# A streaming encoder step on one core: the tiles that TensorE streams, laid out at one offset within 256 bytes

## The chip, the cores and the metric

The kernel runs on one core of one Trainium2 chip, in one launch. The metric is the device time in microseconds. Three runs of the kernel before took 2901.51, 2903.31 and 2903.32 us; the median is 2903.31 us. TensorE multiplies, VectorE (DVE), ScalarE (ACT) and GpSimd (POOL) do the rest, SyncE (SP) issues most DMAs.

## The reference

A two-layer encoder runs on 288 frames: 256 of a new stream (the prompt) and 32 of a running one (the sample), with D = 2048 channels, all in float32.

```python
for i in range(DEPTH):                                   # two layers
    if i % 2 == 0:  h, v = gmlp_mix(x, w_a_in, ..., w_a_out)      # 2048 -> 4096, spatial gating, 2048 -> 2048
    else:           h, s = retention_mix(x, ..., w_b_in, w_b_out) # 2048 -> 12288, 8 heads, 4096 -> 2048
    x = layer_norm(ALPHA * x + h)
    gate, up = jnp.split(x @ w_ffn_in[i], 2, axis=-1)             # 2048 -> 11264
    x = layer_norm(ALPHA * x + (silu(gate) * up) @ w_ffn_out[i])  # 5632 -> 2048
```

Outputs are the frames, the retention states of both streams and the normalised v rows of the sample.

## The kernel before, in words

Activations lie transposed: channels on the 128 partitions, the 288 frames along the free axis. A matrix of 2048 input channels is cut into blocks of 128 x 128; there are `NBLK` = 512 + 256 + 1536 + 512 + 2 x (1408 + 704) = 7040 of them, and 64 blocks of carried state.

Float32 accuracy comes from pairs. Each weight block and each activation tile is split into a rounded part (`hi`) and the rest (`lo`), and `Core.step` (lines 103 to 105) issues three matmuls for a block: `whi` by `xh`, `whi` by `xl`, `wlo` by `xh`. Each loads its 128 x 128 weights and streams 288 columns of the activation. That makes 3 x 7040 = 21120 matmuls. In three places (`PostNorm.start`, `RAW` = 3 groups of 4 output tiles, 16 blocks each) 290 columns are streamed, two of them for the gain and bias of the norm before: 3 x 3 x 4 x 16 x 3 = 1728 matmuls. The other 19392 stream 288 columns.

The stages follow each other: `a_in` (32 output tiles), `a_out` (16), then for each layer `f_in` and `f_out` in two halves, with `b_in` and `b_out` in two halves between the two layers. For an output tile the loop runs over the input tiles `k` (16 for `a_in`, `b_in`, `f_in`, `a_out`, `b_out`; 22 for `f_out`). Only the first group of `a_in` turns this round: for one `k` it runs over 8 output tiles, so 24 matmuls in a row stream the same two tiles `xh[k]` and `xl[k]` (`Core.group`, `lag=0`).

Weights arrive in the order of use, packed in chunks of 8 blocks (512 KB), through SP's queue. For each chunk ACT rounds (`split`, line 413) and DVE subtracts (line 414). Four chunks are held, each block 512 bytes per partition. PE's order is written out by hand; the other engines follow through semaphores, with moves through DRAM issued by POOL (`to_rows`, lines 422 to 424, and `o_move`).

What TensorE streams are: `xh`, `xl` (the input of a mixer or FFN), `g_sh`, `g_sl` (gated product), `hh`, `hl` (FFN hidden half), `r_oh`, `r_ol` (retention output, four tiles for each of four heads). In the built program their rows of 288 or 292 numbers begin, in each partition:

| tile | start, bytes | step from `k` to `k+1` | start of the rows modulo 256 |
|---|---|---|---|
| `xh` | 61568 | 1168 | 128, 16, 160, 48, 192, 80, 224, 112, 0, 144, 32, 176, 64, 208, 96, 240 for k = 0 to 15 |
| `xl` | 80256 | 1168 | the same |
| `g_sh`, `g_sl` | 131712, 150144 | 1152 | 128 and 0 in turn |
| `hh`, `hl` | 131712, 157056 | 1152 | 128 and 0 in turn |
| `r_oh`, `r_ol` | four places each | 1152 | 32 and 160, or 96 and 224, in turn |

The weight blocks `whi` and `wlo` begin at 128 modulo 256 throughout (`whi` at 28800, `wlo` at 45184, blocks 512 and buffers 4096 bytes apart). The first 16384 bytes of each partition are the scratch of the dynamic DMAs.

Of the kernel before, what the change touches and what calls it, by code (L numbers as in the profile page):

```python
# [10 lines left out]
F32 = mybir.dt.float32  # L11
F32R = mybir.dt.float32r
# [7 lines left out]
P = 128  # L20
D = 2048
KT = D // P
NP = 256
NS = 32
NT = NP + NS
NX = NT + 2
ROW = NT + 4
NR = 3 * NS
HID = 5632
HT = HID // P  # L30
HH = HT // 2
# [377 lines left out]
                       lambda m, ps: evac(m, self.correct(m, ps)), lambda s, g=g: hook(g, s))  # L409


def split(nc, hi, lo, f):
    nc.scalar.copy(hi, f)  # L413
    nc.vector.tensor_tensor(lo, f, hi.bitcast(F32), ALU.subtract)  # L414
# [12 lines left out]
def gmlp(core, cst, x, y, lnp, ins, v_out, load):  # L427
    tc, nc = core.tc, core.nc
    xh, xl = x
    xs = lambda k: (xh[:, k, :NT], xl[:, k, :NT])  # L430
    with ExitStack() as es:
        pool = es.enter_context(tc.tile_pool(name="gm", bufs=1, reuse_waits="tile"))
        sh = pool.tile([P, KT, NT], F32R, name="g_sh")
        tv = pool.tile([P, 4, 9, 4, 32], F32, tag="sl", name="g_tv")
        vp = pool.tile([P, 2, D], F32, name="g_vp")
        vs = y.rearrange("p k n -> p (k n)")[:NS, :D]
        v3 = pool.tile([NR, D], F32R, name="g_v3")
# [26 lines left out]
        rows = [P, P, NS]  # L464
# [65 lines left out]
        def mix(m, u):  # L530
            g = m // 2
            ps = core.bank(f"mix{m}")
            for t in range(2):
                nc.tensor.matmul(ps[:, t * P:(t + 1) * P], vp[:, t, m * P:(m + 1) * P], ws[:, g, :], start=True, stop=True)
            s = pool.tile([P, NT], F32, tag="s", name=f"s{m}", bufs=2)
            two = lambda t: t[:, :NP].rearrange("p (t n) -> p t n", t=2)
            nc.vector.tensor_tensor(two(s), two(ps), bs[:, g:g + 1, :].broadcast_to([P, 2, P]), ALU.add)
            nc.vector.tensor_tensor(s[:, NP:], ms[:, m, :], bs[:, g, :NS], ALU.add)
            nc.vector.tensor_tensor(s, s, u, ALU.mult)
            if m == 0:  # L540
                late["sl"] = pool.tile([P, KT, NT], F32R, tag="sl", name="g_sl")
            split(nc, sh[:, m, :], late["sl"][:, m, :], s)

        late = {}
        core.group("a_in", 0, list(range(KT)), list(range(16, 24)), xs, v_evac, load, lag=0)
        core.tiles("a_in", 0, list(range(KT)), list(range(24, 32)), xs, v_evac, grouped=False)
        core.tiles("a_in", 0, list(range(KT)), list(range(16)), xs, u_evac, grouped=False)
        ln = PostNorm(core, cst, x, y, lnp, 0)
        core.tiles("a_out", 0, list(range(KT)), list(range(KT)), lambda k: (sh[:, k, :], late["sl"][:, k, :]),
                   lambda m, ps: ln.last(m, ps, True))  # L550
    return ln

# [1 line left out]
def ffn(core, cst, x, y, lnp, layer, prev, out=None):  # L554
    tc, nc = core.tc, core.nc
    xh, xl = x
    xs = lambda k: (xh[:, k, :NT], xl[:, k, :NT])
    ln = PostNorm(core, cst, x, y, lnp, 2 * layer + 1, out)
    with tc.tile_pool(name=f"ffn{layer}", bufs=1, reuse_waits="tile") as pool:
        hh = pool.tile([P, HH, NT], F32R, name=f"hh{layer}")  # L560
        hl = pool.tile([P, HH, NT], F32R, name=f"hl{layer}")
        for half in range(2):
            sg = {}

            def evac(m, ps):
                if m < HT:
                    t = pool.tile([P, NT], F32, tag="sg", name=f"sg{layer}_{m}", bufs=4)
                    nc.scalar.activation(t, ps[:, :NT], AF.Silu)
                    sg[m] = t
                else:  # L570
                    j = m - HT
                    i = j - half * HH
                    f = pool.tile([P, NT], F32, tag="hf", name=f"hf{layer}_{j}", bufs=3)
                    nc.vector.tensor_tensor(f, ps[:, :NT], sg.pop(j), ALU.mult)
                    split(nc, hh[:, i, :], hl[:, i, :], f)

            ms = []
            for j in range(half * HH, (half + 1) * HH):
                ms += [j, HT + j]
            if half == 0:  # L580
                prev.start(f"f_in{layer}", ms, evac)
                ms = ms[4 * RAW:]
            core.tiles(f"f_in{layer}", 0, list(range(KT)), ms, xs, evac, grouped=False)
            core.tiles(f"f_out{layer}", half * HH, list(range(HH)), list(range(KT)),
                       lambda k: (hh[:, k, :], hl[:, k, :]),
                       ln.last if half else ln.part)
    return ln


def retention(core, cst, x, y, lnp, prev, ins, st_p_out, st_s_out):  # L590
    tc, nc = core.tc, core.nc
    xh, xl = x
    xs = lambda k: (xh[:, k, :NT], xl[:, k, :NT])
    mm = nc.tensor.matmul
    with ExitStack() as es:
        pool = es.enter_context(tc.tile_pool(name="ret", bufs=1, reuse_waits="tile"))
        oh, ol = {}, {}
        cs = pool.tile([P, 2, NT], F32, name="r_cs")
        zt = pool.tile([P, HEADS, 3], F32, name="r_zt")
        inn = pool.tile([P, HEADS, NS], F32, name="r_inn")  # L600
# [8 lines left out]
        heads = {}  # L609

        def pair(name, h):
            t = pool.tile([P, 4 * NT], F32, tag=f"oh{h % 4}", name=name)
            return t[:, :2 * DV].rearrange("p (t f) -> p t f", t=2)

        def rope(dst, a, b, cos, sin, nm):
            t1 = pool.tile([P, NT], F32, tag="rt1", name=f"rt1{nm}", bufs=1)
# [8 lines left out]
        class Head:  # L625
# [10 lines left out]
            def evac(self, m, ps):  # L636
                h = self.h
                if m < 32:
                    self.ps[m % 2] = ps
                    if m % 2:  # L640
                        turn = lambda p=dict(self.ps): self.turn(m, p)
                        if h == 0:
                            core.after(2, turn)
                        else:
                            turn()
                elif m < 64:
                    i = m % 4
                    if i == 0:
                        self.tv = pool.tile([P, 9, 4, 32], F32, tag=f"ol{h % 4}", name=f"tv{h}")
                    nc.vector.transpose(self.tv[:, :, i, :], ps[:, :NT])  # L650
                    if i == 3:
                        self.v_move()
                else:
                    i = m % 4
                    nc.scalar.activation(self.sg[:, i, :], ps[:, :NT], AF.Silu)
                    if i == 3:
                        core.after(1, lambda: self.o_gate("g"))
# [152 lines left out]
            def o_move(self):  # L810
                h = self.h
                to = pair(f"to{h}", h)
                tz = pool.tile([P, DV], F32, tag="tz", name=f"tz{h}")
                self.of = of = pool.tile([P, 9, 4, 32], F32, tag=f"ol{h % 4}", name=f"of{h}")
                nc.vector.transpose(tz[:NS, :], self.ons[:NS, :])
                nc.vector.transpose(to.rearrange("p t f -> p (t f)"), self.onp.rearrange("p t f -> p (t f)"))
                room = core.room([NT, DV], f"o_room{h}")
                nc.gpsimd.dma_start(room[NP:, :], tz[:NS, :])
                nc.gpsimd.dma_start(room[:NP, :].rearrange("(t p) f -> p t f", p=P), to)
                blocks = room.rearrange("(b s) f -> s b f", s=32)  # L820
                for a in range(4):
                    nc.gpsimd.dma_start(of[32 * a:32 * a + 32].rearrange("p b i s -> p b (i s)"), blocks[:, :, a * P:(a + 1) * P])

            def o_gate(self, what):
                self.open.discard(what)
                if self.open:
                    return
                h = self.h
                view = lambda t: t.rearrange("p i (b s) -> p i b s", s=32)
                nc.vector.tensor_tensor(view(self.sg), self.of.rearrange("p b i s -> p i b s"), view(self.sg), ALU.mult)  # L830
                oh[h % 4] = pool.tile([P, 4, NT], F32R, tag=f"oh{h % 4}", name=f"r_oh{h}")
                ol[h % 4] = pool.tile([P, 4, NT], F32R, tag=f"ol{h % 4}", name=f"r_ol{h}")
                for i in range(4):
                    split(nc, oh[h % 4][:, i, :], ol[h % 4][:, i, :], self.sg[:, i, :])

            def states(self):
                h = self.h
# [24 lines left out]
        for grp in range(2):  # L862
            a, b, c, d = order[4 * grp:4 * grp + 4]
            ms = sum(a + b, []) + c[0] + d[0] + c[1] + d[1]
            if grp == 0:
                prev.start("b_in", ms, evac)
                ms = ms[4 * RAW:]
            core.tiles("b_in", 0, list(range(KT)), ms, xs, evac, grouped=False)
            core.tiles("b_out", 16 * grp, list(range(16)), list(range(KT)),
                       lambda k: (oh[k // 4][:, k % 4, :], ol[k // 4][:, k % 4, :]),  # L870
                       ln.last if grp else ln.part)
    return ln

# [2 lines left out]
def hybrid_step(ctx, tc, ins, outs):  # L876
    nc = tc.nc
    ctx.enter_context(tc.manual_schedule(engines={PE}))
    core = Core(ctx, tc, ins["wpack"])
    cp = ctx.enter_context(tc.tile_pool(name="cp", bufs=1))  # L880
    lnp = ctx.enter_context(tc.tile_pool(name="lnp", bufs=1))
    xh = cp.tile([P, KT, ROW], F32R, name="xh")
    xl = cp.tile([P, KT, ROW], F32R, name="xl")
    y = cp.tile([P, KT, NT], F32, name="y")
    cst = {}
    cst["one2048"] = cp.tile([P, P], F32, name="one2048")
# [111 lines left out]
```

## Time and profile before

| | |
|---|---|
| median of three runs | 2903.31 us |
| profiled execution, its own time | 2903.1 us |
| its span | 2901.3 us |
| PE busy | 2888.0 us |
| DVE busy | 1697.5 us |
| ACT busy | 1241.3 us |
| POOL busy | 141.8 us |
| granted TensorE clock, mean | 0.999 of full speed |

The span runs from the first to the last instruction of the profiled execution; 1.8 us of its own time lie outside. Matmuls overlap in the records: each is shown as about 295 ns long, while the next one starts some 130 ns after it. So the busy time of PE says that there was always a matmul under way, not how fast they follow each other. The rate is read from the distance between starts.

### The profile page before, as it was taken

Reading aid. Unit: us, or ns where it says so; the run is one execution under the profiler, and the core shown is the slowest. Engines: PE = TensorE matmul, PEld = TensorE weight load, DVE = VectorE, ACT = ScalarE, POOL = GpSimd, SP = SyncE. Lnnn points to the kernel's source line nnn. Section 1 sums busy time; section 2 is a strip of 40 time slices with the busy share of each in tenths; the row PEclk is TensorE's granted clock in tenths of the full one; section 3 lists DMA queues with packets and bytes.
Section 4 is the critical chain, followed back from the end, with each engine's and each line's share of the span. In section 5 each row is a group of like instructions: output and inputs, shape, how many; then the busy total and the mean of one; then the engine's idle time right before and its main releaser. Section 6 shows DMA issues by size and latency. Waiting matters only on the chain.

```text
span 2901.3 us, 51390 instructions
## 1 busy us (share of the span) xinstructions
PE 2888.0 (100%) x21568; PEld 2873.1 (99%) x21568; DVE 1697.5 (59%) x2432; ACT 1241.3 (43%) x1642; POOL 141.8 (5%) x241
## 2 busy tenths in 40 slices
PE   9999999999999999999999999999999999999998
PEld 9999999999999999999999999999999999999998
DVE  5677864444444456777755566767854444444455
ACT  5444553333333344554443344444543333333343
POOL 1100000000000000012200111200000000000001
PEclk9999999999999999999999999999999999999999
DMA  8654455554555544567655566755454554555553
GB/s 268 209 172 160 160 167 168 167 167 161 166 167 167 167 161 166 185 201 226 221 190 163 191 209 208 219 188 163 165 165 166 167 167 164 165 166 167 167 167 121
DMA packets 146584, 515.49 MB, mean 178 GB/s; under 512 B 18016, under 2 KB 20336, under 8 KB 146320
## 3 DMA queue, kind: packets, MB, share of 16 engines
q1 hardware_dynamic: 131984, 473.47, 49.5%
q0 software_dynamic: 14224, 38.59, 4.6%
q8 instruction: 168, 2.75, 0.4%
q14 instruction: 64, 0.52, 0.1%
q10 hardware_dynamic: 144, 0.15, 0.0%
HBM read 486.98 MB, written 25.17 MB: 177 GB/s over the span
## 4 chain that ended last, share of the span: by engine, by line
PE 98%; DVE 1%; DMA 0%; issue 0%; POOL 0%; ACT 0%; SPq 0%; DVEq 0%; POOLq 0%
PE af_in L104 13%; PE af_in L103 13%; PE af_in L105 13%; PE ab_in L103 7%; PE ab_in L104 7%; PE ab_in L105 7%; PE af_out L103 7%; PE af_out L105 6%; PE af_out L104 6%; PE ab_out L105 2%; PE ab_out L103 2%; PE ab_out L104 2%; PE aa_in L103 2%; PE aa_in L104 2%; PE aa_in L105 2%; PE aa_out L103 1%
## 5 line engine op out<-in xcount | busy, mean ns | idle before, releaser
L414 DVE TENSOR_TENSOR wlo<-raw,whi 128x1024 fp32r<-128x1024 f32 (+1 forms) x892 | 1085.8, 1219 | 951.7 <-ACT whi L413 947.7
L413 ACT CAST whi<-raw 128x1024 fp32r<-128x1024 f32 (+1 forms) x892 | 931.9, 1046 | 1505.7 <-PE af_in L104 353.5
L104 PE MATMUL af_in<-xl,whi 128*128 128x288 f32 (+1 forms) x2816 | 831.4, 295 | 0.0
L103 PE MATMUL af_in<-xh,whi 128*128 128x288 f32 (+1 forms) x2816 | 829.5, 295 | 0.0
L105 PE MATMUL af_in<-xh,wlo 128*128 128x288 f32 (+1 forms) x2816 | 828.0, 294 | 0.0
L103 PEld LDWEIGHTS af_in<-xh,whi 128*128 128x128 f32 x2816 | 530.6, 188 | 0.0
L105 PEld LDWEIGHTS af_in<-xh,wlo 128*128 128x128 f32 x2816 | 530.0, 188 | 0.0
L104 PEld LDWEIGHTS af_in<-xl,whi 128*128 128x128 f32 x2816 | 529.5, 188 | 0.0
L104 PE MATMUL ab_in<-xl,whi 128*128 128x288 f32 (+1 forms) x1536 | 453.3, 295 | 0.0
L103 PE MATMUL ab_in<-xh,whi 128*128 128x288 f32 (+1 forms) x1536 | 453.2, 295 | 0.0
L105 PE MATMUL ab_in<-xh,wlo 128*128 128x288 f32 (+1 forms) x1536 | 451.7, 294 | 0.0
L103 PE MATMUL af_out<-hh,whi 128*128 128x288 f32 x1408 | 416.1, 296 | 0.0
L104 PE MATMUL af_out<-hl,whi 128*128 128x288 f32 x1408 | 415.2, 295 | 0.0
L105 PE MATMUL af_out<-hh,wlo 128*128 128x288 f32 x1408 | 414.4, 294 | 0.0
L103 PEld LDWEIGHTS ab_in<-xh,whi 128*128 128x128 f32 x1536 | 289.2, 188 | 1.0
L104 PEld LDWEIGHTS ab_in<-xl,whi 128*128 128x128 f32 x1536 | 288.9, 188 | 1.1
L105 PEld LDWEIGHTS ab_in<-xh,wlo 128*128 128x128 f32 x1536 | 289.0, 188 | 0.0
L105 PEld LDWEIGHTS af_out<-hh,wlo 128*128 128x128 f32 x1408 | 265.0, 188 | 0.0
L104 PEld LDWEIGHTS af_out<-hl,whi 128*128 128x128 f32 x1408 | 264.3, 188 | 0.0
L103 PEld LDWEIGHTS af_out<-hh,whi 128*128 128x128 f32 x1408 | 263.9, 187 | 0.0
L103 PE MATMUL aa_in<-xh,whi 128*128 128x288 f32 x512 | 152.5, 298 | 0.4 <-ACT xh L413 0.4
L104 PE MATMUL aa_in<-xl,whi 128*128 128x288 f32 x512 | 152.0, 297 | 0.0
(253 smaller groups left out, 2941.1 us busy)
## 6 DMA issues: line engine op xcount, KB each, us to landing
raw<-in_wpack_dram SPq DMA_DIRECT2D x887, 512.0 KB, 3.4
v_room<-tv POOLq DMA_DIRECT2D x32, 144.0 KB, 4.8
of<-o_room POOLq DMA_DIRECT2D x32, 144.0 KB, 4.4
vw<-v_room POOLq DMA_DIRECT2D x8, 512.0 KB, 6.1
out_st_s_dram<-sso POOLq DMA_DIRECT2D x16, 256.0 KB, 2.8
o_room<-to POOLq DMA_DIRECT2D x8, 512.0 KB, 3.6
out_st_p_dram<-so POOLq DMA_DIRECT2D x16, 256.0 KB, 5.2
y<-in_xT_dram SPq DMA_DIRECT2D x8, 288.0 KB, 5.3
```

The costliest lines, as they stand in the source:

```text
L103: mm(ps[:, :n], hi, xh, start=first, stop=False)
L104: mm(ps[:, :n], hi, xl, start=False, stop=False)
L105: mm(ps[:, :n], lo, xh, start=False, stop=last)
L413: nc.scalar.copy(hi, f)
L414: nc.vector.tensor_tensor(lo, f, hi.bitcast(F32), ALU.subtract)
```

## The change

The tiles that TensorE streams are now allocated by one helper, `moving`. Each row takes 320 numbers (1280 bytes, a multiple of 256) instead of 288 or 292, and the data begin 4 numbers (16 bytes) after the row's start. A small tile (`shift`) puts `xh` on a multiple of 256. In retention eight tiles of 4 x 320 numbers are reserved first, so that they lie on multiples of 256 too; the intermediate tiles that share their room are made as long. The scratch of the dynamic DMAs goes from 16384 to 8192 bytes per partition.

In the built program `xh` is then at 53504, `xl` at 73984, `hh` at 127232, `hl` at 155392, and the retention tiles at 127232 and every 5120 bytes after it: all multiples of 256, with the data 16 bytes further on. Weight blocks stay at 128 modulo 256. On every engine the instructions and their order are the same as before; some ten waits name another semaphore, as tiles share other room.

```diff
-ROW = NT + 4
+ROW = 320
+LEAD = 4
...
+def moving(pool, n, name, tag=None):
+    t = pool.tile([P, n, ROW], F32R, name=name, **({"tag": tag} if tag else {}))
+    return t[:, :, LEAD:]
...
-        sh = pool.tile([P, KT, NT], F32R, name="g_sh")
-        tv = pool.tile([P, 4, 9, 4, 32], F32, tag="sl", name="g_tv")
+        sh = moving(pool, KT, "g_sh")
+        tv = pool.tile([P, KT * ROW], F32, tag="sl", name="g_tv")
+        tv = tv[:, :KT * NT].rearrange("p (q b i s) -> p q b i s", q=4, b=9, i=4)
...
-                late["sl"] = pool.tile([P, KT, NT], F32R, tag="sl", name="g_sl")
-            split(nc, sh[:, m, :], late["sl"][:, m, :], s)
+                late["sl"] = moving(pool, KT, "g_sl", "sl")
+            split(nc, sh[:, m, :NT], late["sl"][:, m, :NT], s)
...
-        hh = pool.tile([P, HH, NT], F32R, name=f"hh{layer}")
-        hl = pool.tile([P, HH, NT], F32R, name=f"hl{layer}")
+        hh = moving(pool, HH, f"hh{layer}")
+        hl = moving(pool, HH, f"hl{layer}")
...
+        for i in range(8):
+            pool.tile([P, 4 * ROW], F32, tag=f"o{'hl'[i % 2]}{i // 2}", name=f"r_room{i}")
...
-                oh[h % 4] = pool.tile([P, 4, NT], F32R, tag=f"oh{h % 4}", name=f"r_oh{h}")
-                ol[h % 4] = pool.tile([P, 4, NT], F32R, tag=f"ol{h % 4}", name=f"r_ol{h}")
+                oh[h % 4] = moving(pool, 4, f"r_oh{h}", f"oh{h % 4}")
+                ol[h % 4] = moving(pool, 4, f"r_ol{h}", f"ol{h % 4}")
...
-    xh = cp.tile([P, KT, ROW], F32R, name="xh")
-    xl = cp.tile([P, KT, ROW], F32R, name="xl")
+    cp.tile([P, 32], F32, name="shift")
+    xh = moving(cp, KT, "xh")
+    xl = moving(cp, KT, "xl")
...
-    nc = _bacc.Bacc("TRN2", target_bir_lowering=False, num_devices=1)
+    nc = _bacc.Bacc("TRN2", target_bir_lowering=False, num_devices=1, dynamic_dma_scratch_size=8192)
```

## Rows read from the trace of the kernel before

**Rows 1.** Page, part 1: busy us of each engine, share of span, instructions.

```profile
PE 2888.0 (100%) x21568; PEld 2873.1 (99%) x21568; DVE 1697.5 (59%) x2432; ACT 1241.3 (43%) x1642; POOL 141.8 (5%) x241
```

**Rows 2.** Page, part 4: shares of the chain of work that ended last.

```profile
PE 98%; DVE 1%; DMA 0%; issue 0%; POOL 0%; ACT 0%; SPq 0%; DVEq 0%; POOLq 0%
```

**Rows 3.** Waits of TensorE: us in total, times, longest us.

```profile
PE smix L519 <- DVE g_v L414: 1.1, 1, 1.1
PE warm L893 <- POOL g_nrm L461: 1.0, 1, 1.0
PE aa_in L103 <- ACT xh L413: 0.4, 1, 0.4
```

**Rows 4.** Page, part 5: the two operations that split each weight chunk.

```profile
L414 DVE TENSOR_TENSOR wlo<-raw,whi 128x1024 fp32r<-128x1024 f32 (+1 forms) x892 | 1085.8, 1219 | 951.7 <-ACT whi L413 947.7
L413 ACT CAST whi<-raw 128x1024 fp32r<-128x1024 f32 (+1 forms) x892 | 931.9, 1046 | 1505.7 <-PE af_in L104 353.5
```

**Rows 5.** Windows: stretch, its us, busy us (count) per engine, TensorE clock, DMA share, GB/s.

```profile
5.00:60.00 55.00, 54.86 (x396) 54.65 (x397) 34.14 (x54) 31.01 (x50) 0.05 (x1) 1.00 0.81 276
400.00:600.00 200.00, 200.00 (x1517) 200.00 (x1516) 94.48 (x109) 79.21 (x104) 0.00 (x0) 1.00 0.51 166
1160.00:2050.00 890.00, 890.00 (x6545) 877.89 (x6545) 600.71 (x973) 407.36 (x554) 115.24 (x198) 1.00 0.61 196
```

**Rows 6.** Timeline of TensorE (start us, us, ...): first matmul of each stage, layer 0.

```profile
322.45 0.30 PE L103 MATMUL af_in<-xh,whi 128*128 128x290 f32 x1
...
400.27 0.29 PE L103 MATMUL af_in<-xh,whi 128*128 128x288 f32 x1
...
603.15 0.29 PE L103 MATMUL af_out<-hh,whi 128*128 128x288 f32 x1
...
743.73 0.30 PE L103 MATMUL af_in<-xh,whi 128*128 128x288 f32 x1
...
1022.71 0.29 PE L103 MATMUL af_out<-hh,whi 128*128 128x288 f32 x1
```

**Rows 7.** Timeline of TensorE, first group of `a_in`: starts at some values of `k`.

```profile
10.74 0.30 PE L103 MATMUL aa_in<-xh,whi 128*128 128x288 f32 x1
...
11.28 0.29 PE L104 MATMUL aa_in<-xl,whi 128*128 128x288 f32 x1
...
13.88 0.29 PE L103 MATMUL aa_in<-xh,whi 128*128 128x288 f32 x1
...
17.08 0.29 PE L103 MATMUL aa_in<-xh,whi 128*128 128x288 f32 x1
...
20.23 0.29 PE L103 MATMUL aa_in<-xh,whi 128*128 128x288 f32 x1
...
45.68 0.29 PE L103 MATMUL aa_in<-xh,whi 128*128 128x288 f32 x1
...
48.87 0.29 PE L103 MATMUL aa_in<-xh,whi 128*128 128x288 f32 x1
...
52.02 0.29 PE L103 MATMUL aa_in<-xh,whi 128*128 128x288 f32 x1
...
55.21 0.29 PE L103 MATMUL aa_in<-xh,whi 128*128 128x288 f32 x1
...
58.43 0.29 PE L103 MATMUL aa_in<-xh,whi 128*128 128x288 f32 x1
```

**Rows 8.** Timeline, all engines: the move of `k` of head 0, and its reader.

```profile
1253.85 2.44 POOL L422 DMA_DIRECT2D k_room<-tk  x4 [23.81 <-DVE tk L689]
1259.49 0.76 POOL L423 DMA_DIRECT2D kw<-k_room  x1 [3.21 <-DMA k_room<-tk]
...
1264.86 0.91 ACT L703 ACTIVATE kh<-kw,r_zt 128x256 fp32r<-128x256 f32 x2 [0.28 <-DMA kw<-k_room]
1265.67 1.03 ACT L709 ACTIVATE ks<-kw,r_zt 32x256 fp32r<-32x256 f32 x2
...
1275.77 0.64 PE L770 MATMUL ss<-vs,ks 96*128 96x512 f32 x2
```

More of the change, by code (lines that the diff above doesn't have):

```diff
@@ L548, in gmlp @@
         ln = PostNorm(core, cst, x, y, lnp, 0)
-        core.tiles("a_out", 0, list(range(KT)), list(range(KT)), lambda k: (sh[:, k, :], late["sl"][:, k, :]),
+        core.tiles("a_out", 0, list(range(KT)), list(range(KT)), lambda k: (sh[:, k, :NT], late["sl"][:, k, :NT]),
                    lambda m, ps: ln.last(m, ps, True))
@@ L574, in evac @@
                     nc.vector.tensor_tensor(f, ps[:, :NT], sg.pop(j), ALU.mult)
-                    split(nc, hh[:, i, :], hl[:, i, :], f)
+                    split(nc, hh[:, i, :NT], hl[:, i, :NT], f)
             ms = []
@@ L584, in ffn @@
             core.tiles(f"f_out{layer}", half * HH, list(range(HH)), list(range(KT)),
-                       lambda k: (hh[:, k, :], hl[:, k, :]),
+                       lambda k: (hh[:, k, :NT], hl[:, k, :NT]),
                        ln.last if half else ln.part)
@@ L611, in pair, with blocks @@
         def pair(name, h):
-            t = pool.tile([P, 4 * NT], F32, tag=f"oh{h % 4}", name=name)
+            t = pool.tile([P, 4 * ROW], F32, tag=f"oh{h % 4}", name=name)
             return t[:, :2 * DV].rearrange("p (t f) -> p t f", t=2)
+        def blocks(name, h):
+            t = pool.tile([P, 4 * ROW], F32, tag=f"ol{h % 4}", name=name)
+            return t[:, :4 * NT].rearrange("p (b i s) -> p b i s", b=9, i=4)
         def rope(dst, a, b, cos, sin, nm):
@@ L648, in evac @@
                     if i == 0:
-                        self.tv = pool.tile([P, 9, 4, 32], F32, tag=f"ol{h % 4}", name=f"tv{h}")
+                        self.tv = blocks(f"tv{h}", h)
                     nc.vector.transpose(self.tv[:, :, i, :], ps[:, :NT])
@@ L813, in o_move @@
                 tz = pool.tile([P, DV], F32, tag="tz", name=f"tz{h}")
-                self.of = of = pool.tile([P, 9, 4, 32], F32, tag=f"ol{h % 4}", name=f"of{h}")
+                self.of = of = blocks(f"of{h}", h)
                 nc.vector.transpose(tz[:NS, :], self.ons[:NS, :])
@@ L819, in o_move @@
                 nc.gpsimd.dma_start(room[:NP, :].rearrange("(t p) f -> p t f", p=P), to)
-                blocks = room.rearrange("(b s) f -> s b f", s=32)
+                rows = room.rearrange("(b s) f -> s b f", s=32)
                 for a in range(4):
-                    nc.gpsimd.dma_start(of[32 * a:32 * a + 32].rearrange("p b i s -> p b (i s)"), blocks[:, :, a * P:(a + 1) * P])
+                    nc.gpsimd.dma_start(of[32 * a:32 * a + 32].rearrange("p b i s -> p b (i s)"), rows[:, :, a * P:(a + 1) * P])
             def o_gate(self, what):
@@ L830, in o_gate @@
                 nc.vector.tensor_tensor(view(self.sg), self.of.rearrange("p b i s -> p i b s"), view(self.sg), ALU.mult)
-                oh[h % 4] = pool.tile([P, 4, NT], F32R, tag=f"oh{h % 4}", name=f"r_oh{h}")
-                ol[h % 4] = pool.tile([P, 4, NT], F32R, tag=f"ol{h % 4}", name=f"r_ol{h}")
+                oh[h % 4] = moving(pool, 4, f"r_oh{h}", f"oh{h % 4}")
+                ol[h % 4] = moving(pool, 4, f"r_ol{h}", f"ol{h % 4}")
                 for i in range(4):
-                    split(nc, oh[h % 4][:, i, :], ol[h % 4][:, i, :], self.sg[:, i, :])
+                    split(nc, oh[h % 4][:, i, :NT], ol[h % 4][:, i, :NT], self.sg[:, i, :])
             def states(self):
@@ L869, in retention @@
             core.tiles("b_out", 16 * grp, list(range(16)), list(range(KT)),
-                       lambda k: (oh[k // 4][:, k % 4, :], ol[k // 4][:, k % 4, :]),
+                       lambda k: (oh[k // 4][:, k % 4, :NT], ol[k // 4][:, k % 4, :NT]),
                        ln.last if grp else ln.part)
```

## The prediction, made before the changed kernel ran

> **What bounds the kernel now.** I read the page's busy times first, then the chain of waits, then the waits of TensorE, then the timeline for the distance between its matmuls. PE is busy for 2888.0 of 2901.3 us [rows 1], the chain that ended last is 98% PE [rows 2], and PE waited for others for 2.5 us in the whole run [rows 3]. So no transfer and no other engine sets the time; what sets it is how fast matmuls follow each other. The splits of a weight chunk, which take 1.22 us on DVE and 1.05 us on ACT [rows 4], fit well into the 24 matmuls (some 3.2 us) for which a chunk lasts. Even in retention, the busiest stretch of DVE, it works 600.71 of 890 us [rows 5].
>
> The distance between starts comes out of the first matmuls of the stages [rows 6]. `f_in` with 288 columns begins at 400.27 and is followed by `f_out` at 603.15: 22 pairs of output tiles less the 6 pairs in the 290-column groups, so 32 tiles x 48 = 1536 matmuls in 202.88 us, 132.1 ns each. The second half has 44 tiles, 2112 matmuls, from 743.73 to 1022.71: 132.1 ns again. `f_out` has 16 x 66 = 1056 from 603.15 to 743.73: 133.1 ns. The 290-column groups take 77.82 us from 322.45 for 576 matmuls and four small ones of the norm: 134.2 ns.
>
> [...]
>
> **What the rows say on addresses.** The first group of `a_in` is a natural experiment: for one `k`, 24 matmuls in a row stream tiles at one offset modulo 256, then the next `k` has another. The first matmuls of k = 1, 2, 3, 4 are at 10.74, 13.88, 17.08 and 20.23 us, those of k = 12 to 15 at 45.68, 48.87, 52.02 and 55.21, and 58.43 is the next output tile [rows 7]. The differences, divided by 24:
>
> - k = 1, offset 16: 3.14 us, 130.8 ns
> - k = 2, offset 160: 3.20 us, 133.3 ns
> - k = 3, offset 48: 3.15 us, 131.3 ns
> - k = 12, offset 64: 3.19 us, 132.9 ns
> - k = 13, offset 208: 3.15 us, 131.3 ns
> - k = 14, offset 96: 3.19 us, 132.9 ns
> - k = 15, offset 240: 3.22 us, 134.2 ns
>
> All of k = 1 to 15 take 47.69 us for 360, 132.5 ns, the same as `f_in`, in which all offsets take turns. Starts are rounded to 0.01 us, so a difference over 24 is good to some 0.4 ns: offset 16 is the lowest, 240 the highest. At offset 16 the first few matmuls still differ (10.74 to 11.28 us holds four, 135 ns each); the 20 from 11.28 to 13.88 us take 2.60 us, 130.0 ns. In those 20 the weight block moves on through the chunk and `xh` and `xl` alternate, which lie differently modulo 1024 (272 and 528). The spacing doesn't follow either. So I take 130.0 ns as the state into which a long run at offset 16 against weights at offset 128 settles. In the changed kernel nearly all of the program is one such run.
>
> **The change part by part.**
>
> *Tiles of 288 columns.* Those of `a_in`, `b_in` and `f_in` without the 290-column groups number 1536 + 4032 + 7296 = 12864, and at 132.1 ns come to 1699.3 us; those of `a_out`, `b_out` and `f_out` number 768 + 1536 + 4224 = 6528, and at 133.1 ns come to 868.9 us. Together they are 19392. At 130.0 ns they take 2521.0 us: 47.2 us less. The stages that I have no rows for go at the value of their kind.
>
> *Groups of 290 columns.* No row shows them at one offset. From above they stay at 134.2 ns (231.9 us); from below they come down as far as the least value seen, 130.0 ns (224.6 us). [...]
>
> *Other matmuls* (retention's of 512 columns, the norms') stream tiles of another kind. Their offsets move too, as tiles around them do. There are some 450 records of them; at the widest spread above, 134.2 - 130.0 ns, that is 2 us either way. I take nothing.
>
> *The writers of these tiles.* ACT and DVE write the same numbers, contiguous within a row; only the step between rows grows. No row shows a step of 1280. Were each of these writes longer, PE would not see it: a chunk takes 3.12 us at the new rate, against 1.22 us on DVE, and the other work of DVE leaves a third of retention free [rows 5]. The weights' transfers would have to come 2% faster. In `f_in` the DMA share is 0.51; only in the first 55 us is it 0.81 [rows 5], where 1.1 us is all that a faster PE would ask for. Cost nothing.
>
> *Half the scratch for POOL's DMAs.* If a move found no room, it would go out later. The closest reader I find is the retention `k` of a head: its four DMAs to DRAM start at 1253.85 us, the one back at 1259.49, ACT has scaled it at 1266.70 and PE reads it at 1275.77 [rows 8]. So 9 us of slack cover it. The trace shows no move waiting for room, so its price lies between nothing and whatever exceeds 9 us; I take nothing.
>
> The sum: 47.2 + 5.9 = 53.1 us, made against the profiled execution's 2903.1 us, which leaves 2850.0 us. The median of the runs shown is 2903.31, 0.2 us from that, so the forecast for a timed run is 2850 us.
>
> [...]
>
> **The rivals.**
>
> *The settled spacing depends on higher address bits.* For it: only two places of the tiles modulo 1024 (272 and 528) were seen at offset 16, while the new rows step through four. Against it: in the 20 matmuls above, weights at both places modulo 1024 and tiles at two gave one spacing. If half of the rows fall back to the average over offsets, half of the gain stays: 2903 - 27 = 2877 us.
>
> *Nothing changes.* The differences in rows 7 would belong to `k`'s place in the first 60 us (transfers are dense there), not to offsets. For it: `f_out`, which knows two offsets only, takes 133.1 ns, close to the rest. Against it: k = 13 is fast late in the same stretch, between two slow ones. Time 2903 us. [...]
>
> *The run settles in a slow cycle.* [...] Place: every stage, most of all `f_in` (7296 matmuls). For it: k = 15 stays at 134.2 ns for 24 matmuls. Against it: offset 16 itself settled lowest. [...] It decides as soon as the settled spacing is above 132.6 ns, the present mean (2800.1 us / 21120).
>
> *The scratch.* To eat up the gain, each of eight heads would have to be 9 + 53/8 = 15.6 us late. I give it no share of its own beside the slow cycle.
>
> **How the numbers follow.** 0.68 for the forecast, whose own range is 2838 to 2862 (spacing 129.5 to 130.5 ns, and the 290-column bounds); 0.15 for the half gain at 2877; 0.08 for no change; 0.09 for the slow cycle at 2939. The range from 2836 to 2884 takes in the forecast and most of the half gain and leaves the last two out. A measurement of this kernel can tell about 0.2% (6 us) from no change; so faster is 0.83, the same 0.08, slower 0.09.
>
> **What would show it.** Right: in the changed trace `f_in`'s 1536 and 2112 matmuls take 199.7 and 274.6 us from first to first, `f_out`'s 1056 take 137.3 us, all at 130.0 ns, with no difference between the two kinds of stage; PE's waits stay at a few us, and POOL's moves in retention keep their distance from their readers. Wrong: spacing that differs by `k` or by stage (the higher bits count), spacing of 132 to 133 ns (offset is not the cause), or above 132.6 ns (a slow cycle). Idle time of PE in retention would point at the scratch.

## The result and the profile after

The changed kernel takes 2861.56 us (median of 4 runs, 2860.01 to 2865.03) against 2903.32 us (4 runs, 2901.51 to 2905.20). The ratio is 0.9858, 95% interval 0.9841 to 0.9875: 1.4% faster, 11.6 us slower than the forecast of 2850 and inside its range. The profiled execution took 2865.03 us, with a span of 2863.2 us.

The page after first (busy times, shares of the chain, the two splits), then the waits of TensorE: what stood in [rows 1 to 4].

```profile
PE 2848.8 (99%) x21568; PEld 2834.2 (99%) x21568; DVE 1697.4 (59%) x2432; ACT 1239.9 (43%) x1642; POOL 141.4 (5%) x241
...
PE 98%; DVE 1%; DMA 0%; issue 0%; POOL 0%; ACT 0%; SPq 0%; DVEq 0%; POOLq 0%
...
L421 DVE TENSOR_TENSOR wlo<-raw,whi 128x1024 fp32r<-128x1024 f32 (+1 forms) x892 | 1085.7, 1219 | 919.3 <-ACT whi L420 915.5
L420 ACT CAST whi<-raw 128x1024 fp32r<-128x1024 f32 (+1 forms) x892 | 931.1, 1045 | 1461.5 <-PE af_in L105 349.8
```

```profile
PE smix L527 <- DVE g_v L421: 1.6, 1, 1.6
PE aa_in L104 <- ACT xh L420: 1.0, 1, 1.0
PE warm L908 <- POOL g_nrm L469: 1.0, 1, 1.0
```

TensorE is still the chain, and it waits 3.6 us instead of 2.5. DVE, ACT and POOL are as busy as before. So the 38 us are in the distance between matmuls. The windows (columns as in [rows 5]) show the same granted clock, 1.00, and more matmuls in the same time: 1528 for 1517, and 6614 for 6545.

```profile
400.00:600.00 200.00, 200.00 (x1528) 200.00 (x1527) 91.81 (x99) 77.37 (x96) 0.00 (x0) 1.00 0.52 171
1160.00:2050.00 890.00, 890.00 (x6614) 878.19 (x6614) 613.02 (x998) 414.19 (x566) 112.17 (x191) 1.00 0.61 197
```

The timeline of TensorE after: first matmuls of stages as in [rows 6], those of layer 1 too (from 2096.75), and three of the single matmuls with which the norm centres its input (`cen`, L260).

```profile
316.63 0.29 PE L104 MATMUL af_in<-xh,whi 128*128 128x290 f32 x1
...
393.96 0.30 PE L104 MATMUL af_in<-xh,whi 128*128 128x288 f32 x1
...
595.35 0.29 PE L104 MATMUL af_out<-hh,whi 128*128 128x288 f32 x1
...
733.80 0.29 PE L104 MATMUL af_in<-xh,whi 128*128 128x288 f32 x1
...
1010.71 0.29 PE L104 MATMUL af_out<-hh,whi 128*128 128x288 f32 x1
...
1053.97 0.29 PE L260 MATMUL cen<-cen,one_r 128*128 128x288 f32 x1
...
1148.49 0.29 PE L104 MATMUL ab_in<-xh,whi 128*128 128x290 f32 x1
...
1950.63 0.29 PE L260 MATMUL cen<-cen,one_r 128*128 128x288 f32 x1
...
2096.75 0.29 PE L104 MATMUL af_in<-xh,whi 128*128 128x288 f32 x1
...
2296.44 0.29 PE L104 MATMUL af_out<-hh,whi 128*128 128x288 f32 x1
...
2433.72 0.29 PE L104 MATMUL af_in<-xh,whi 128*128 128x288 f32 x1
...
2708.28 0.29 PE L104 MATMUL af_out<-hh,whi 128*128 128x288 f32 x1
...
2751.19 0.29 PE L260 MATMUL cen<-cen,one_r 128*128 128x288 f32 x1
```

| stretch, matmuls | before, us | forecast | after, layer 0 | after, layer 1 |
|---|---|---|---|---|
| `f_in`, first half, 1536 | 202.88 | 199.7 | 201.39 (131.1 ns) | 199.69 (130.0 ns) |
| `f_out`, first half, 1056 | 140.58 | 137.3 | 138.45 (131.1 ns) | 137.28 (130.0 ns) |
| `f_in`, second half, 2112 | 278.98 | 274.6 | 276.91 (131.1 ns) | 274.56 (130.0 ns) |
| 290 columns, 576 and 4 small | 77.82 | 75.9 | 77.33 (133.3 ns) | |

The forecast is met to 0.1 us in layer 1 and missed in layer 0. In the trace's nanoseconds two patterns of distances between starts repeat: 131, 129, in places 130, 130 (a cycle of two, 130.0 ns each), and 130, 132 or 133, 130 or 131 (a cycle of three, 131.1 ns each). Tiles, weights and offsets are the same in both. The spacing changes at a matmul of another kind: 1010.71 to 1053.97 holds 330 matmuls of 131.1 ns, and from the `cen` at 1053.97 to 1148.49 the other 726, with the `cen` itself, have 130.0. In the other direction it goes at the `cen` at 247.28 us and 2751.19; the `cen` at 1950.63 leads back to 130.0. In retention it goes back and forth with each head: after the score matmuls (`sc`) and again after `ss` 48 matmuls of `b_in` have 130.0 ns, and from the matmuls of `ob` on it is 131.1 until the next head's `sc`. Of the second head, 48 matmuls from 1325.00 (6.24 us) and 240 from 1342.36 (31.47 us):

```profile
1325.00 0.30 PE L104 MATMUL ab_in<-xh,whi 128*128 128x288 f32 x1
...
1331.24 0.40 PE L809 MATMUL ob<-vh,ph 128*128 128x512 f32 x1
...
1342.36 0.29 PE L104 MATMUL ab_in<-xh,whi 128*128 128x288 f32 x1
...
1373.83 1.03 PE L733 MATMUL sc<-rq,rk 128*128 128x256 f32 x4
```

The first group of `a_in` no longer differs by `k` [rows 7]: 369 matmuls from the first row, in k = 1, to the second, 24 matmuls past k = 15, 130.0 ns each.

```profile
11.22 0.29 PE L104 MATMUL aa_in<-xh,whi 128*128 128x288 f32 x1
...
59.19 0.29 PE L104 MATMUL aa_in<-xh,whi 128*128 128x288 f32 x1
```

The move of `k` of head 0 [rows 8]: ACT reads it 5.25 us after the issue (5.37 before) and is done at 1252.85. PE's reader now starts at 1259.87, 7.0 us later, where it was 9.1: nearer by 2 us, and still not late.

```profile
1245.76 0.75 POOL L430 DMA_DIRECT2D kw<-k_room  x1 [3.50 <-DMA k_room<-tk]
...
1251.01 0.91 ACT L717 ACTIVATE kh<-kw,r_zt 128x256 fp32r<-128x256 f32 x2 [2.17 <-DMA kw<-k_room]
```

### The profile page after: what moved, and what is told of

Same layout as the page of the kernel before. It is cut to its first block, busy times and chain, and to the rows that moved or that the text cites. A ratio compares the mean times of both kernels' runs of the same rounds, so it can differ in the third digit from the quotient of the medians.

```text
span 2863.2 us, 51389 instructions
## 1 busy us (share of the span) xinstructions
PE 2848.8 (99%) x21568; PEld 2834.2 (99%) x21568; DVE 1697.4 (59%) x2432; ACT 1239.9 (43%) x1642; POOL 141.4 (5%) x241
## 4 chain that ended last, share of the span: by engine, by line
PE 98%; DVE 1%; DMA 0%; issue 0%; POOL 0%; ACT 0%; SPq 0%; DVEq 0%; POOLq 0%
PE af_in L105 13%; PE af_in L104 13%; PE af_in L106 13%; PE ab_in L105 7%; PE ab_in L104 7%; PE ab_in L106 7%; PE af_out L105 6%; PE af_out L104 6%; PE af_out L106 6%; PE ab_out L105 2%; PE ab_out L104 2%; PE ab_out L106 2%; PE aa_in L105 2%; PE aa_in L106 2%; PE aa_in L104 2%; PE aa_out L105 1%
## 5 line engine op out<-in xcount | busy, mean ns | idle before, releaser
L421 DVE TENSOR_TENSOR wlo<-raw,whi 128x1024 fp32r<-128x1024 f32 (+1 forms) x892 | 1085.7, 1219 | 919.3 <-ACT whi L420 915.5
L420 ACT CAST whi<-raw 128x1024 fp32r<-128x1024 f32 (+1 forms) x892 | 931.1, 1045 | 1461.5 <-PE af_in L105 349.8
L105 PE MATMUL ab_out<-r_ol,whi 128*128 128x288 f32 x512 | 150.8, 294 | 0.0
```

The source lines that it names most:

```text
L105: mm(ps[:, :n], hi, xl, start=False, stop=False)
```

## The experiments

Each kernel is the changed one with the edit shown, unless the text says otherwise. A kernel that was run once is set against the kernel before on the same chip.

**The scratch alone.** The kernel before, run once and then timed, with

```diff
-    nc = _bacc.Bacc("TRN2", target_bir_lowering=False, num_devices=1)
+    nc = _bacc.Bacc("TRN2", target_bir_lowering=False, num_devices=1, dynamic_dma_scratch_size=8192)
```

> The kernel before with the scratch of the dynamic DMAs halved and nothing else. All tiles move by 8192 bytes, so no offset modulo 256 changes. My theory (the gain is the offset of the tiles, the scratch costs nothing): 2903 us, spacing of f_in 132.1 ns and of f_out 133.1 ns as before, PE waits of a few us. Rival (the scratch costs what the change fell short of the forecast, 12 us): 2915 us, with idle time of PE in retention.

2906.39 us against 2901.09. The spacing is that of before, but PE's wait for `g_v` is 4.0 us where it was 1.1. Behind it is a load: DVE waits 3.21 us for `g_vp`, where it waited 0.33 us in the kernel before. After PE's wait the granted clock is 0.50 for 6.8 us, from 134.7 us, and 17 matmuls start 240 ns apart; the kernel before shows neither there.

```profile
PE smix L519 <- DVE g_v L414: 4.0, 1, 4.0
```

```profile
125.48 1.29 DVE L481 BATCH_NORM_STATS2 g_st<-g_vp 128x6 f32<-128x512 f32 x2 [3.21 <-DMA g_vp<-g_room]
```

Was that the scratch, or does this load vary by itself? Hence the timed repeat:

> The kernel before with the halved scratch alone, now timed in rounds: its single run was 5.3 us over the kernel before, with one wait of PE for the v rows at 128 us that was 2.9 us longer. Theory (the landing time of that transfer varies from run to run, the scratch costs nothing): within 2 us of the kernel before. Rival (the scratch delays it): 4 to 6 us slower in every round.

2902.54 us (11 runs) against 2902.81, ratio 1.000 (0.9991 to 1.0009), and the wait was 1.4 us. The scratch costs nothing. The load's landing varies: in the kernels with the smaller scratch the wait was 0.2 to 2.0 us in all but this run and one below.

**The same regular layout at offset 0.** `LEAD = 4` becomes `LEAD = 0`.

> The changed kernel with the data at the start of each 1280-byte row (offset 0 instead of 16 modulo 256), weights at 128. Theory A (the offset sets a cycle of its own): as in the group of k = 8 of the kernel before, which ran at offset 0 with 133.3 ns, so some 2.7 ns more than the changed kernel, about 2914 us. Theory B (one constant offset is enough, whichever it is): 2861 us.

2919.02 us against 2901.09: slower than before. `f_in`'s 1536 matmuls from 400.69 to 605.50 are 133.3 ns each, and so are `f_out`'s 1056. One offset for all is no gain by itself; 16 is.

```profile
400.69 0.30 PE L104 MATMUL af_in<-xh,whi 128*128 128x288 f32 x1
...
605.50 0.29 PE L104 MATMUL af_out<-hh,whi 128*128 128x288 f32 x1
...
746.30 0.29 PE L104 MATMUL af_in<-xh,whi 128*128 128x288 f32 x1
```

**Weights moved, tiles kept.** The weights go from 128 to 160 modulo 256, the tiles stay at 16.

```diff
+        self.wp.tile([P, 8], F32, name="wshift", bufs=1)
...
-    cp.tile([P, 32], F32, name="shift")
+    cp.tile([P, 24], F32, name="shift")
```

> The changed kernel with tiles still at 16 and the weight blocks moved from 128 to 160 modulo 256. Theory A1 (what counts is the distance between tile and weights): this is the distance of a tile at 240 with weights at 128, which took 134.2 ns, so about 2931 us. Theory A2 (the tile's own offset counts, weights don't): 2861 us.

2924.14 us against 2901.09. The 768 matmuls of `b_out`'s first half take 103.43 us, 134.7 ns, and `f_in` stands at 133.3 (399.42 to 604.21, 1536 matmuls). The tiles did not move, so the weights are a partner. The new distance, 16 - 160 = 112 modulo 256, is that of k = 15 in the kernel before (240 - 128), the slowest of [rows 7] with 134.2 ns. The pattern is the same too: 126 or 127, 143 or 144, 138 or 139, 130, 135 ns repeats over the last 16 matmuls of that k and over `b_out`.

```profile
399.42 0.29 PE L105 MATMUL af_in<-xh,whi 128*128 128x288 f32 x1
...
604.21 0.29 PE L105 MATMUL af_out<-hh,whi 128*128 128x288 f32 x1
...
1510.77 0.29 PE L105 MATMUL ab_out<-r_oh,whi 128*128 128x288 f32 x1
...
1614.20 0.29 PE L105 MATMUL ab_in<-xh,whi 128*128 128x288 f32 x1
```

**Both moved by 32 bytes.** The same, with `LEAD = 12`: weights at 160, tiles at 48.

> Weights at 160 and tiles at 48 modulo 256: both 32 bytes further than in the changed kernel, the distance as there. Theory A1 (distance): 2861 us, with the two cycles of 130.0 and 131.1 ns. Theory A2 (the tile's own offset): the 131.3 ns that k = 3 took at offset 48 in the kernel before, some 2875 us, and another pattern of spacings.

2864.79 us against 2901.09. `f_in` repeats the change's spacing: 201.39 us for its first half in layer 0 and 199.69 us in layer 1, to the hundredth. So 130.0 and 131.1 belong to the distance between tile and weights, not to either's own position. Which of the two holds is not repeated everywhere: after the `cen` at 1056.00 the 726 matmuls of `f_out` have 131.1 ns (130.0 in the change), and most of `b_in` and `b_out` has 130.0 (131.1 in the change).

```profile
395.98 0.29 PE L105 MATMUL af_in<-xh,whi 128*128 128x288 f32 x1
...
597.37 0.29 PE L105 MATMUL af_out<-hh,whi 128*128 128x288 f32 x1
...
2097.05 0.29 PE L105 MATMUL af_in<-xh,whi 128*128 128x288 f32 x1
...
2296.74 0.29 PE L105 MATMUL af_out<-hh,whi 128*128 128x288 f32 x1
```

```profile
1056.00 0.29 PE L261 MATMUL cen<-cen,one_r 128*128 128x288 f32 x1
...
1151.32 0.30 PE L105 MATMUL ab_in<-xh,whi 128*128 128x290 f32 x1
```

That the distance counts modulo 256 and not 128 is seen in the kernel before: k = 1 and k = 9, at 16 and 144, take 130.0 and 131.7 ns over their last 20 matmuls, and k = 15 and k = 7, at 240 and 112, take 134.7 and 131.8.

**The centring matmul at the same distance.** The norm's `one_r` goes to 128 modulo 256 and its moving row through `moving`; room for it comes from a scratch of 4096 bytes.

```diff
-            r = self.tmp("cen", F32R)
+            r = moving(lnp, 1, f"cenr_{gi}", "cenr")[:, 0, :NT]
...
+    cp.tile([P, 32], F32, name="shift1")
...
```

> The changed kernel, whose norm's single centring matmul now also streams a tile at 16 modulo 256 against weights at 128 (one_r moved from 0 to 128, the rounded row in a 1280-byte tile of its own; scratch 4096 bytes for the room). In the changed kernel the spacing jumps between a cycle of two (130.0 ns) and a cycle of three (131.1 ns) at this matmul. Theory C (a matmul at another distance is what throws the run from one cycle into the other): the run stays in the cycle of two past the norms, 2851 us or somewhat more where retention's own matmuls still disturb it. Rival (the cycles change at other places or by chance): 2861 us.

2867.11 us (4 runs), ratio 0.9875 (0.9859 to 0.9892): not the 2851 expected, and no faster than the change. The jump at the `cen` is gone: 1012.88 to 1055.78 holds 330 matmuls of 130.0 ns, and 130.0 it stays to 1150.29. All of `f_in` and `f_out` with 288 columns is at 130.0. But `a_in` starts out in the cycle of three, and the last 528 matmuls of `a_out`, most of `b_in` and all of `b_out` are in it. The wait for `g_v` is 4.5 us, with the granted clock at 0.50 for 6.8 us behind it, as in the run with the scratch alone. So what a foreign matmul streams, or from where, can decide the cycle; retention's matmuls were left alone. Whether the small scratch has a part in the wait is open.

```profile
1012.88 0.29 PE L104 MATMUL af_out<-hh,whi 128*128 128x288 f32 x1
...
1055.78 0.29 PE L260 MATMUL cen<-cenr,one_r 128*128 128x288 f32 x1
...
1150.29 0.29 PE L104 MATMUL ab_in<-xh,whi 128*128 128x290 f32 x1
```

**Fewer weights read.** The correction by `wlo` is left out for three quarters of the outputs, and the order of the three matmuls changes.

```diff
-        mm(ps[:, :n], hi, xl, start=False, stop=False)
-        mm(ps[:, :n], lo, xh, start=False, stop=last)
+        mm(ps[:32, :n], lo[:, :32], xh, start=False, stop=False)
+        mm(ps[:, :n], hi, xl, start=False, stop=last)
```

> The changed kernel with one of three weight loads, wlo, cut to 32 of its 128 columns (the correction by wlo is left out for three quarters of the outputs) and this matmul moved between the other two. [...]

2882.93 us against 2902.20, slower than the change. A third of the matmuls load a quarter of the columns, yet `f_in`'s 1536 take 202.08 us, 131.6 ns. The change has 131.1 ns there, so the spacing is not in proportion to what is loaded. How much of the 131.6 belongs to the new order is not shown, as no run changes the order alone.

```profile
396.65 0.29 PE L104 MATMUL af_in<-xh,whi 128*128 128x288 f32 x1
...
598.73 0.29 PE L104 MATMUL af_out<-hh,whi 128*128 128x288 f32 x1
```

**Many offsets in one kernel.** The input of each second matrix gets offsets of its own for `hi` and `lo`, another pair for the first values of `k` than for the rest.

```diff
+COMBOS = [(1, 1), (2, 2), (3, 3), (5, 5), (6, 6), (7, 7), (10, 10), (14, 14), (4, 12), (12, 4), (4, 28), (28, 4), (4, 32), (12, 28)]
+def at(t, c, k, w):
+    a = COMBOS[c][w]
+    return t[:, k, a:a + NT]
...
```

> The changed kernel with xh and xl as they are, and other pairs of offsets (hi tile, lo tile, in bytes past a multiple of 256) in the second matrices: 4, 8, 12, 20, 24, 28, 40, 56 for both, and 16/48, 48/16, 16/112, 112/16, 16/128, 48/112; two pairs in each half of f_out and b_out and in a_out, so that each is read from its own stretch. Theory A1 (distance sets a cycle) expects each stretch to settle at a spacing of its own between 127 and 135 ns. [...] If the pair counts beside the distance, 16/48 and 48/16 differ from the mean of 130.0 and 131.5 ns.

2877.71 us against 2902.20. The mean spacing of each pair, the first nine matmuls after a change left out, in bytes past a multiple of 256 (weights at 128):

| both at | ns | `hi`, `lo` at | ns |
|---|---|---|---|
| 28 | 130.0 | 48, 16 | 131.2 |
| 40 | 130.0 | 16, 128 | 131.2 |
| 56 | 133.1 | 16, 112 | 131.3 |
| 4, 12, 24 | 133.3 to 133.4 | 16, 48 | 132.1 |
| 8 | 136.0 | 48, 112 | 133.3 |
| 20 | 140.0 | 112, 16 | 135.6 |

In the timeline, 33 matmuls at 12 bytes from the first row to the second (4.40 us, 133 ns), then 33 at 20 bytes (4.61 us, 140 ns); further down 33 at 40 bytes (4.30 us, 130 ns).

```profile
669.63 0.30 PE L111 MATMUL af_out<-hh,whi 128*128 128x288 f32 x1
...
674.03 0.29 PE L111 MATMUL af_out<-hh,whi 128*128 128x288 f32 x1
...
678.64 0.30 PE L111 MATMUL af_out<-hh,whi 128*128 128x288 f32 x1
...
2384.60 0.30 PE L111 MATMUL af_out<-hh,whi 128*128 128x288 f32 x1
...
2388.90 0.30 PE L111 MATMUL af_out<-hh,whi 128*128 128x288 f32 x1
```

Steps of 4 bytes count: 20, 24 and 28 give 140.0, 133.3 and 130.0. None is below 130.0.

**The two good offsets for all tiles**, `LEAD = 10` (40 bytes) and `LEAD = 7` (28 bytes), the second run once and then timed. The weights stay at 128 in all of them; the 0 in the last expectation is a slip.

> The changed kernel with all tiles at 40 instead of 16 modulo 256, weights at 128. In the probe of offsets the stretch at 40 for both tiles ran at 130, 130, 130 ns in all of its 13 passes, although each began out of another pair's stretch. Theory D (at 40 the run always falls back into 130.0 ns): all stages with 288 columns at 130.0 ns, no jump at norms or in retention, about 12 us less than the changed kernel, 2850 us; the 290-column groups at 131 to 134 ns. Rival (the second cycle appears here too once the run is long): 2861 us.

> The changed kernel with all tiles at 28 modulo 256, where the probe showed 131 and 129 ns in turn in all 13 passes. Theory D: 130.0 ns in all stages, 2850 us. Rival (as at 16, a second cycle exists and retention's other matmuls throw the run into it): 2855 to 2861 us.

> The tiles 28 bytes past a multiple of 256 (the weights at 0), timed. If the distance alone sets the spacing, all stages of 288 columns stand at 130.0 ns without a jump, as in the look at this offset (2852.6 us), and the median comes out within 3 us of the kernel at offset 40 (2855.8 us), so 2852 to 2858 us. Rival: that the look was one of the better executions, and the wait for g_v at about 128 us decides between the two offsets; then the median is 2855 to 2860 us, and the wait is over 3 us in the profile.

and beside the first, on the same chip, the change once more:

> The changed kernel itself, on the chip of this comparison: 2861.5 us again, with the cycles of 130.0 and 131.1 ns in the same stages if other matmuls decide which holds, in other stages if chance does.

| kernel | median, us (range) | ratio (interval) |
|---|---|---|
| offset 40 | 2855.80 (2854.15 to 2862.19) | 0.9842 (0.9828 to 0.9855) |
| the change again, offset 16 | 2860.89 (2859.43 to 2864.87) | 0.9857 (0.9844 to 0.9871) |
| offset 28, run once | 2852.57 | |
| offset 28, timed later on another chip | 2854.70 (2852.89 to 2858.57) | 0.9834 (0.9821 to 0.9848) |

At both offsets no matmul of another kind leads to a second cycle that stays. The timeline of the timed kernel at offset 28 has in layer 0 what the change has only in layer 1: 1536 matmuls in 199.68 us, 1056 in 137.28.

```profile
392.59 0.29 PE L104 MATMUL af_in<-xh,whi 128*128 128x288 f32 x1
...
592.27 0.29 PE L104 MATMUL af_out<-hh,whi 128*128 128x288 f32 x1
...
729.55 0.29 PE L104 MATMUL af_in<-xh,whi 128*128 128x288 f32 x1
```

The change run again changes cycle at the same places as before, so that is no chance of one execution. There is one exception: 96 matmuls of `a_in`, from 132.63 us after the first `smix`, take 131.1 ns where the first execution had 130.0. Both better offsets beat the kernel before; against the change the intervals overlap, but three of four runs at 40 and all of those at 28 lie below all of the change's. The profiled executions differ by 10.0 us (2864.87 and 2854.87), near the 12 expected, the medians by 5.1: the change's two profiled executions were the slowest of their four, and no trace shows which cycles the others were in.

## Why the prediction was right, and where its sizes were off

*What bounds the kernel*: right. The whole gain lies in the distance between matmuls, at an unchanged clock (1.00 in the windows), with an unchanged chain (98% PE).

*Offsets set that distance*: right, and more exactly than it was put. The weights were assumed to be the partner; 32 bytes on them alone undid the gain (2924.14 us against the change's profiled 2865.03, 59 us more), 32 bytes on both brought it back (2864.79 us). It is the distance that counts, modulo 256.

*130.0 ns as the settled state at offset 16*: right as a state, wrong as the only one. The step that was mis-sized is the sentence that the changed kernel is nearly all one such run. 20 matmuls could not show a second cycle at the same distance, nor that the norm's or retention's matmuls lead into it. That they showed 130.0 was in part luck: in the run with the scratch alone the same k = 1 takes 131.05 ns over its last 20 matmuls and ends in the cycle of three. By the trace of the change 10,368 matmuls lie in that cycle (528 of `a_out`, 3648 of `f_in`, 1386 and 726 of `f_out`, 3072 of `b_in`, 1008 of `b_out`). At 1.11 ns each (393.3 / 3 - 130.0) that is 11.5 us of the 47.2 that did not come. Offsets 28 and 40, without that cycle, bear it out.

*290 columns*: mis-sized. The 5.9 us of the forecast put these 1728 matmuls at 130.8 ns, 0.8 ns over the settled 130.0 for two more columns, and no run shows that step. 133.3 ns came (77.33 us for 576 and 4 small ones), just inside the upper bound of 134.2. Over 1728 matmuls the gain was 1.4 us, not 5.9: 4.4 us short. So 290 columns took 3.3 ns more than the 130.0 of 288; 133.3 stood at offsets 16, 28 and 40 alike, and with the weights at 160 it was 131.1 in the groups of `f_in` in both layers and 133.3 in those of `b_in`. So the best distance may be another for this length.

The two add up to 15.9 us. PE's waits take 1.1 us more than before, and the first 24 matmuls, 16 of which started 240 ns apart before, take 3.6 us instead of 5.6. That leaves 15.0 us, by which the profiled execution is above the forecast. The median of the timed runs is 3.5 us lower still, and no trace says which of the terms is smaller there.

The forecast's own range has a slip: its terms (9.7 us either way for the spacing, 1.4 less or 5.9 more for 290 columns) give 2839 to 2866, not 2838 to 2862. The median of 2861.56 is inside both. And the 132.5 ns over all of k = 1 to 15 are near `f_in`'s 132.1, not the same.

*Costs taken as nothing*: right. The splits take 1219 and 1045 ns as before (1219 and 1046), and the scratch alone has ratio 1.000.

*Rivals.* Higher address bits: not the cause; in layer 1 rows at all their places run at 130.0, and the cycles move with the distance. But half the gain lost was the right kind of worry: a quarter was lost, to another mechanism. Nothing changes: refuted. A slow cycle: real, at other distances. The layout at offset 0 came out at 2919 us and with weights at 160 at 2924 us, slower than before, and only the offset chosen, 16, kept the change from it; 134.2 ns throughout (21120 x 134.2 ns) would be 34 us more than the 2800.1 us of before, 2937 us, near the 2939 of the prediction. The scratch: refuted.

Open is what in the chip makes the distance count, why 130.0 ns is the least seen at a granted clock of 1.00, and what makes a cycle stay or go.

## What to carry to other kernels

Where TensorE is the chain, look for the same matmul with operands at other addresses in the trace one has: the spacing by `k` (130.8 to 134.2 ns) was worth 1.4% here. Then scan the distance from tile to weights in steps of 4 bytes with one kernel that holds many offsets, for each length of row, and time the best alone, since a regular layout at a bad distance was worse than the mixed one here (2919.02 and 2924.14 us against 2901.09). Before a settled value goes into a forecast, ask what else runs between such stretches: it may lead to another cycle.

## What was not expected of the hardware

- One instruction stream at one distance has two stable cycles, 130.0 and 131.1 ns, for thousands of matmuls, and a single other matmul can switch them, at the same places in two executions but for 96 matmuls.
- The cycles that repeat cleanly last 260, 393.3, 400 and (at offset 0: 133, 132, 133, 136) 533.3 ns, and 140.0 at offset 20: all multiples of 6.67 ns (39, 59, 60, 80 and 21 times that).
- 4 bytes cost 6.7 ns a matmul (140.0 ns at 20 against 133.3 at 24). Offsets 28 and 40 keep the 130.0 ns that 16 has only in part, so a multiple of 16 is not what counts.
